# Mean over rows of 32 KiB: one load queue with one row per descriptor, in place of two queues with two adjacent rows per descriptor

## The chip, the cores and the metric

The kernel runs on one NeuronCore of a Trainium2 chip. The metric is the device time of one execution in microseconds (us); for the kernel before it is 1252.54 us, the median of three runs (1252.18 to 1252.76). The engines are named as in the profile: DVE is VectorE, ACT is ScalarE, SP is SyncE, PE is TensorE, POOL is GpSimd; a name with a q (SPq, ACTq) is an engine's instruction queue, and PEld is TensorE's weight load. DMA queue q1 carries what SyncE issues, q10 what ScalarE issues.

## The reference

The input `x` has the shape 64 x 256 x 8192 in float32 (536.87 MB). The output is the mean over the last axis, 64 x 256 values:

```python
def reference(x):
    return np.mean(x, axis=2)
```

Seen as a matrix, there are 16,384 rows of 8192 numbers (32 KiB each), and each row gives one number. Every input byte is read once and used in one addition.

## The kernel before, in words

The rows are cut into NB = 64 blocks of 256 rows, 8 MiB each. A block is a tile `xt` of 128 partitions x R = 2 rows x 8192 columns. The view `x_v` says which row goes where: with `(n p r) s -> n p r s`, partition p of block n holds rows 2p and 2p+1 of the block, which are adjacent in memory, so that one partition's share is a single run of 64 KiB.

**Bulk.** LB = 63 blocks go through a pool of three buffers (`BULK_BUFS`). `load(n)` (line 71) issues one DMA for a whole block, on SyncE's queue for even n and on ScalarE's for odd n. Three loads are issued ahead; after that, load n+3 is issued right after the two sums of block n, whose buffer it takes. `dve_sum` (line 61, a VectorE tensor_reduce) sums row 0 of each partition into a column of `res[0]`; `act_sum` (line 64, a ScalarE activation with an accumulator that writes its copy back over the input) sums row 1 into a column of `res[1]`. A load into a used buffer waits for both sums of the block that was there.

**Last block.** It uses a fourth turn of the same pool. Row 0 of all partitions is one DMA (line 91, 4 MiB); its left half is summed on VectorE and its right half on ScalarE, into the two columns of `head`. Row 1 is loaded in chunks of 4096, 2048, 1024 and 512 columns (line 97), each halved between the two engines, whose sums go to columns of `fin_in`; the last 512 columns are loaded straight into `fin_in` (line 106) behind the others on SyncE's queue.

**Results.** Line 108 multiplies the two parts of `head` by 1/8192 and adds them up, into `fin`. The 63 columns of `res[0]` and `res[1]` are each transposed on TensorE (line 121) and scaled into `bulk` on VectorE (line 122), and stored with one DMA (line 123) issued by SyncE. Line 125 scales the last 512 columns and the eight partial sums beside them and adds them up on VectorE, and line 134 stores the last block's 256 means.

The framework that builds the program orders the instructions of each engine itself, and so a line of the source can run earlier than its place: on VectorE one of the two operations of line 122 runs ahead of the sum of `head`, the other behind it, and the sums of the chunks follow line 108. Within an engine's queue the order is then fixed, and an instruction that waits holds up those behind it.

Of the kernel before, what the change touches and what calls it, by code (L numbers as in the profile page):

```python
# [1 line left out]

# [4 lines left out]

ROWS = 2
BULK_BUFS = 3
LAST_CHUNKS = (4096, 2048, 1024, 512, 512)  # L10


@with_exitstack
def kernel(
    ctx: ExitStack,
    tc: tile.TileContext,
    x: bass.AP,
    out: bass.AP,
):
    nc = tc.nc  # L20
    P = nc.NUM_PARTITIONS
    F32 = mybir.dt.float32
    X = mybir.AxisListType.X
    ADD = mybir.AluOpType.add
    COPY = mybir.ActivationFunctionType.Copy

    B, C, S = x.shape
    N = B * C
    R = ROWS
    assert R == 2 and N % (P * R) == 0, (N, P, R)  # L30
    NB = N // (P * R)
    LB = NB - 1
    assert 1 <= LB <= P and sum(LAST_CHUNKS) == S
    inv = 1.0 / float(S)

    x_v = x.rearrange("b c s -> (b c) s").rearrange("(n p r) s -> n p r s", p=P, r=R)
    o_v = out.rearrange("b c -> (b c)")
    out_bulk = o_v[0 : LB * P * R].rearrange("(n p r) -> n p r", p=P, r=R)
    out_last = o_v[LB * P * R : N].rearrange("(p r) -> p r", r=R)

    in_pool = ctx.enter_context(tc.tile_pool(name="in", bufs=BULK_BUFS))
    res_pool = ctx.enter_context(tc.tile_pool(name="res", bufs=1))
    psum_pool = ctx.enter_context(
        tc.tile_pool(name="psum", bufs=1, space=bass.MemoryType.PSUM)
    )

    res = [res_pool.tile([P, NB], F32, name=f"res{r}") for r in range(R)]
    ident = res_pool.tile([P, P], F32)
    nc.gpsimd.memset(ident[:], 0.0)  # L49
    nc.gpsimd.affine_select(  # L50
        out=ident[:],
        in_=ident[:],
        compare_op=mybir.AluOpType.not_equal,
        fill=1.0,
        base=0,
        pattern=[[-1, P]],
        channel_multiplier=1,
    )

    def dve_sum(dst, src):  # L60
        nc.vector.tensor_reduce(out=dst, in_=src, axis=X, op=ADD)  # L61

    def act_sum(dst, src):
        nc.scalar.activation(out=src, in_=src, func=COPY, accum_out=dst)  # L64

    queues = [nc.sync, nc.scalar]
    loaded = {}

    def load(n):
        xt = in_pool.tile([P, R, S], x.dtype, name="xt")  # L70
        queues[n % 2].dma_start(out=xt[:], in_=x_v[n])
        loaded[n] = xt

    for n in range(min(BULK_BUFS, LB)):
        load(n)
    for n in range(LB):
        xt = loaded.pop(n)
        dve_sum(res[0][:, n : n + 1], xt[:, 0, :])
        act_sum(res[1][:, n : n + 1], xt[:, 1, :])
        if n + BULK_BUFS < LB:  # L80
            load(n + BULK_BUFS)

    nparts = 2 * len(LAST_CHUNKS)
    lastw = LAST_CHUNKS[-1]
    xl = in_pool.tile([P, R, S], x.dtype, name="xt")
    fin_in = res_pool.tile([P, lastw + nparts], F32)
    fin = res_pool.tile([P, R], F32)
    head = res_pool.tile([P, 2], F32)

    half = S // 2  # L90
    nc.sync.dma_start(out=xl[:, 0, :], in_=x_v[LB, :, 0, :])
    dve_sum(head[:, 0:1], xl[:, 0, 0:half])
    act_sum(head[:, 1:2], xl[:, 0, half:S])

    pos, k = 0, 0
    for c, w in enumerate(LAST_CHUNKS[:-1]):
        ld = nc.sync.dma_start(
            out=xl[:, 1, pos : pos + w], in_=x_v[LB, :, 1, pos : pos + w]
        )
        mid = pos + w // 2  # L100
        dve_sum(fin_in[:, lastw + k : lastw + k + 1], xl[:, 1, pos:mid])
        act_sum(fin_in[:, lastw + k + 1 : lastw + k + 2], xl[:, 1, mid : pos + w])
        k += 2
        pos += w
    with tc.issue_after(ld.ins):
        nc.sync.dma_start(out=fin_in[:, 0:lastw], in_=x_v[LB, :, 1, pos:S])

    nc.vector.tensor_scalar(  # L108
        out=head[:],
        in0=head[:],  # L110
        scalar1=inv,
        scalar2=None,
        op0=mybir.AluOpType.mult,
        op1=ADD,
        accum_out=fin[:, 0:1],
    )

    bulk = res_pool.tile([P, P, R], F32)
    for r in range(R):
        ps = psum_pool.tile([P, P], F32, name=f"ps{r}")  # L120
        nc.tensor.transpose(out=ps[:LB, :], in_=res[r][:, 0:LB], identity=ident[:])  # L121
        nc.vector.tensor_scalar_mul(out=bulk[:LB, :, r], in0=ps[:LB, :], scalar1=inv)  # L122
    nc.sync.dma_start(out=out_bulk, in_=bulk[:LB])

    nc.vector.tensor_scalar(  # L125
        out=fin_in[:, 0 : lastw + k],
        in0=fin_in[:, 0 : lastw + k],
        scalar1=inv,
        scalar2=None,
        op0=mybir.AluOpType.mult,  # L130
        op1=ADD,
        accum_out=fin[:, 1:2],
    )
    nc.sync.dma_start(out=out_last, in_=fin[:])


# [1 line left out]
_INS = ['x']  # L138
_OUTS = [((64, 256), 'float32')]


# [23 lines left out]
```

## Time and profile before

| what | value |
|---|---|
| median of three runs | 1252.54 us |
| the profiled execution's own time | 1252.76 us |
| its span, first to last instruction | 1251.0 us |
| VectorE busy | 555.6 us (44%) |
| ScalarE busy | 457.8 us (37%) |
| one sum of 8192 columns on VectorE | 8.684 us, 63 of them |
| one sum of 8192 columns on ScalarE | 7.030 us, 63 of them |
| VectorE waiting for loads | 690.4 us |
| ScalarE waiting for loads | 782.5 us |
| DMA packets | 10156, 536.97 MB, 429 GB/s over the span |
| queue q1 (SyncE) | 5688 packets, 276.89 MB |
| queue q10 (ScalarE) | 4464 packets, 260.05 MB |
| a bulk load on SyncE, issue to landing | 39.6 us (median of 32) |
| a bulk load on ScalarE, issue to landing | 36.2 us (median of 31) |
| the last store, issue to landing | 3.3 us |

How to read it: "busy" is the time in which an engine executes; waiting for a load is idle time that ended with a DMA's landing. The time from issue to landing holds the wait behind earlier transfers and the sharing with the other queue, not only the transfer. A packet is one piece that one of the 16 DMA engines moves; the share of a DMA queue is the time that its packets took, over the time of 16 engines. The difference between the profiled execution's time and its span, 1.76 us, lies around the program.

### The profile page before, as it was taken

What the parts mean: (1) busy time and instruction counts of PE and PEld (TensorE: products, weight loads), DVE (VectorE), ACT (ScalarE), POOL (GpSimd) and SP (SyncE); (2) the same over time, 40 slices, a digit from 0 to 9 for tenths busy, and PEclk for the clock granted to TensorE, in tenths of its full rate; (3) what the DMA queues carried; (4) which work ended last, traced back from release to release, by engine and by line L of the source; (5) the groups of instructions that cost most, each with busy time, mean ns of one, the idle gap of its engine ahead of it and who ended that gap; (6) DMA issues with size and microseconds to landing.
All of it is one profiled execution on the core that took longest, in us unless ns stands there. A gap on an engine that the chain in (4) does not pass through costs nothing. (4 is left out here: it accounts for less than half of the span.)

```text
span 1251.0 us, 434 instructions
## 1 busy us (share of the span) xinstructions
PE 0.7 (0%) x2; PEld 0.3 (0%) x2; DVE 555.6 (44%) x74; ACT 457.8 (37%) x137; POOL 0.7 (0%) x6
## 2 busy tenths in 40 slices
PE   0000000000000000000000000000000000000000
PEld 0000000000000000000000000000000000000000
DVE  0525543345433455333553335543255432555338
ACT  0424432234422344322443224442244422444226
POOL 0000000000000000000000000000000000000000
DMA  9999999999999999999999999999999999999997
GB/s 402 436 436 436 436 436 436 436 436 423 423 427 436 436 436 436 436 436 436 436 436 434 436 427 423 425 436 436 436 436 436 436 434 436 434 434 436 436 419 294
DMA packets 10156, 536.97 MB, mean 429 GB/s; under 512 B 1257, under 2 KB 1320, under 8 KB 1704
## 3 DMA queue, kind: packets, MB, share of 16 engines
q1 hardware_dynamic: 5688, 276.89, 51.3%
q10 hardware_dynamic: 4464, 260.05, 48.1%
q14 instruction: 4, 0.03, 0.0%
HBM read 536.87 MB, written 0.07 MB: 429 GB/s over the span
## 5 line engine op out<-in xcount | busy, mean ns | idle before, releaser
L61 DVE TENSOR_REDUCE res<-xt 128x1 f32<-128x8192 f32 x63 | 545.7, 8684 | 690.4 <-DMA xt<-in_x_dram 690.4
L64 ACT ACTIVATE xt<-xt 128x8192 f32<-128x8192 f32 (+2 forms) x68 | 450.5, 6625 | 784.5 <-DMA xt<-in_x_dram 782.5
L64 ACT ACTIVATION_READ_ACCUMULATOR xt<-xt 128x1 f32 x68 | 12.7, 187 | 0.0
L61 DVE TENSOR_REDUCE head<-xt 128x1 f32<-128x4096 f32 x1 | 4.4, 4402 | 0.0
L61 DVE TENSOR_REDUCE fin_in<-xt 128x1 f32<-128x2048 f32 (+3 forms) x4 | 4.3, 1144 | 0.0
L64 ACT ACT_TABLE_LOAD x1 | 1.3, 1283 | 1.2 <-PEq L149 1.2
L121 PE MATMUL ps<-ident,res 128*63 128x128 f32 x2 | 0.7, 433 | 1236.3 <-DVE res L61 1236.3
L122 DVE TENSOR_SCALAR bulk<-ps 63x128 f32<-63x128 f32 x2 | 0.6, 278 | 0.6 <-PE ps L121 0.6
L125 DVE TENSOR_SCALAR_CACHE_REDUCE fin_in<-fin_in 128x520 f32<-128x520 f32 x1 | 0.7, 694 | 0.1
L121 PEld LDWEIGHTS ps<-ident,res 128*63 128x63 f32 x2 | 0.3, 205 | 1236.3 <-issue 1236.3
L50 POOL TENSOR_SCALAR_AFFINE_SELECT ident<-ident 128x128 f32<-128x128 f32 x1 | 0.3, 294 | 0.1
L49 POOL MEMSET ident<- 128x128 f32 x1 | 0.2, 205 | 0.3 <-POOLq L149 0.3
L108 DVE TENSOR_SCALAR_CACHE_REDUCE head<-head 128x2 f32<-128x2 f32 x1 | 0.2, 155 | 0.0
L149 POOL MEMSET const-bfloat16-1.0<- 128x1 bf16 x1 | 0.1, 102 | 0.0
L149 POOL MEMSET const-uint8-127<- 128x1 uint8 x1 | 0.1, 102 | 0.0
L149 POOL MEMSET const-float32-0.0<- 128x1 f32 x1 | 0.1, 99 | 0.2 <-issue 0.2
L149 POOL MEMSET const-float32-1.0<- 128x1 f32 x1 | 0.1, 99 | 0.0
L108 DVE DVE_READ_ACCUMULATOR head<-head 128x1 f32 x1 | 0.1, 83 | 0.0
L125 DVE DVE_READ_ACCUMULATOR fin_in<-fin_in 128x1 f32 x1 | 0.1, 82 | 0.0
## 6 DMA issues: line engine op xcount, KB each, us to landing
xt<-in_x_dram SPq DMA_DIRECT2D x1, 4096.0 KB, 35.0
xt<-in_x_dram SPq DMA_DIRECT2D x1, 2048.0 KB, 39.5
xt<-in_x_dram SPq DMA_DIRECT2D x1, 1024.0 KB, 41.6
xt<-in_x_dram SPq DMA_DIRECT2D x32, 39.6
xt<-in_x_dram SPq DMA_DIRECT2D x1, 512.0 KB, 42.4
xt<-in_x_dram ACTq DMA_DIRECT2D x31, 36.2
xt<-in_x_dram SPq DMA_DIRECT2D x1, 256.0 KB, 42.5
fin_in<-in_x_dram SPq DMA_DIRECT2D x1, 256.0 KB, 42.7
```

The costliest lines, as they stand in the source:

```text
L49: nc.gpsimd.memset(ident[:], 0.0)
L50: nc.gpsimd.affine_select(out=ident[:], in_=ident[:], compare_op=mybir.AluOpType.not_equal, fill=1.0, base=0, pattern=[[-1, P]], channel_m ...
L61: nc.vector.tensor_reduce(out=dst, in_=src, axis=X, op=ADD)
L64: nc.scalar.activation(out=src, in_=src, func=COPY, accum_out=dst)
L108: nc.vector.tensor_scalar(out=head[:], in0=head[:], scalar1=inv, scalar2=None, op0=mybir.AluOpType.mult, op1=ADD, accum_out=fin[:, 0:1],)
L121: nc.tensor.transpose(out=ps[:LB, :], in_=res[r][:, 0:LB], identity=ident[:])
L122: nc.vector.tensor_scalar_mul(out=bulk[:LB, :, r], in0=ps[:LB, :], scalar1=inv)
L125: nc.vector.tensor_scalar(out=fin_in[:, 0 : lastw + k], in0=fin_in[:, 0 : lastw + k], scalar1=inv, scalar2=None, op0=mybir.AluOpType.mult, ...
L149: nc = _bacc.Bacc("TRN2", target_bir_lowering=False, num_devices=1)
```

## The change

The view of the input becomes `(n r p) s -> n p r s`: partition p of a block holds rows p and 128+p, two runs of 32 KiB that lie 4 MiB apart. The views of the output follow. All loads are issued by SyncE; the load of a block stands in the loop ahead of its two sums, and the three buffers alone decide how far ahead of the sums it is issued. `bulk` becomes 128 x 2 x 128 with the row index outside, so that line 122 writes contiguous columns. The chunks of the last block, the sums and the number of buffers stay.

```diff
-    x_v = x.rearrange("b c s -> (b c) s").rearrange("(n p r) s -> n p r s", p=P, r=R)
+    x_v = x.rearrange("b c s -> (b c) s").rearrange("(n r p) s -> n p r s", p=P, r=R)
     o_v = out.rearrange("b c -> (b c)")
-    out_bulk = o_v[0 : LB * P * R].rearrange("(n p r) -> n p r", p=P, r=R)
-    out_last = o_v[LB * P * R : N].rearrange("(p r) -> p r", r=R)
+    out_bulk = o_v[0 : LB * P * R].rearrange("(n r p) -> n r p", p=P, r=R)
+    out_last = o_v[LB * P * R : N].rearrange("(r p) -> p r", r=R)
...
-    queues = [nc.sync, nc.scalar]
-    loaded = {}
-
-    def load(n):
+    for n in range(LB):
         xt = in_pool.tile([P, R, S], x.dtype, name="xt")
-        queues[n % 2].dma_start(out=xt[:], in_=x_v[n])
-        loaded[n] = xt
-
-    for n in range(min(BULK_BUFS, LB)):
-        load(n)
-    for n in range(LB):
-        xt = loaded.pop(n)
+        nc.sync.dma_start(out=xt[:], in_=x_v[n])
         dve_sum(res[0][:, n : n + 1], xt[:, 0, :])
         act_sum(res[1][:, n : n + 1], xt[:, 1, :])
-        if n + BULK_BUFS < LB:
-            load(n + BULK_BUFS)
...
-    bulk = res_pool.tile([P, P, R], F32)
+    bulk = res_pool.tile([P, R, P], F32)
...
-        nc.vector.tensor_scalar_mul(out=bulk[:LB, :, r], in0=ps[:LB, :], scalar1=inv)
+        nc.vector.tensor_scalar_mul(out=bulk[:LB, r, :], in0=ps[:LB, :], scalar1=inv)
```

## The prediction

> **What bounds the kernel now.** I read the page's 40 slices and queues first, then the chain of waits, the timeline of the tail, and last the DMA packets of two short windows in which one queue is alone.
>
> The slices and the queues say what the span is made of:
>
> ```profile
> DMA  9999999999999999999999999999999999999997
> ...
> HBM read 536.87 MB, written 0.07 MB: 429 GB/s over the span
> ```
>
> The DMA engines are never idle; VectorE is busy 44% and ScalarE 37%, and both stand waiting for loads (690.4 and 782.5 us). The stream's steady rate is read from the timeline of VectorE:
>
> ```profile
> 1141.47 17.28 DVE L61 TENSOR_REDUCE res<-xt 128x1 f32<-128x8192 f32 x2 [20.34 <-DMA xt<-in_x_dram]
> ...
> 1177.77 8.69 DVE L61 TENSOR_REDUCE res<-xt 128x1 f32<-128x8192 f32 x1 [19.01 <-DMA xt<-in_x_dram]
> ...
> 1189.86 8.69 DVE L61 TENSOR_REDUCE res<-xt 128x1 f32<-128x8192 f32 x1 [3.40 <-DMA xt<-in_x_dram]
> ...
> 1218.89 17.28 DVE L61 TENSOR_REDUCE res<-xt 128x1 f32<-128x8192 f32 x2 [20.35 <-DMA xt<-in_x_dram]
> ```
>
> Four blocks take 77.42 us, 19.35 us each. The pattern is uneven because two queues share the engines: two blocks come close together ("x2" is two sums without a gap), then one, then one. The last such pair is at the very end, and there it costs something. The chain that ended last is short:
>
> ```profile
> 1245.05 0.92 DVE fin_in L61 x2
> 1245.97 0.11 issue
> 1246.08 0.69 DVE fin_in L125
> ```
>
> These are sums on VectorE, not a transfer. The last chunk (issued at 1200.89, 42.7 us to landing) was there at 1243.59, so L125 starts 2.49 us after its data:
>
> ```profile
> 1237.01 4.40 DVE L61 TENSOR_REDUCE head<-xt 128x1 f32<-128x4096 f32 x1
> ...
> 1241.64 4.33 DVE L61 TENSOR_REDUCE fin_in<-xt 128x1 f32<-128x2048 f32 x4
> ```
>
> VectorE is behind: blocks 61 and 62 keep it until 1236.2, so `head`, whose row landed at 1233.62, starts at 1237.01, and four sums run without a gap.
>
> The change sets the size of a packet, so its price is needed. Queue lines give packets, MB and the share of 16 engines' time. First the 64 KiB packets between 42 and 50 us, SyncE's queue alone, then the 32 KiB packets of the last block's first row between 1223 and 1227.9 us:
>
> ```profile
> q1 hardware_dynamic: 48, 3.15, 90.8%
> ```
>
> ```profile
> q1 hardware_dynamic: 64, 2.06, 97.8%
> ```
>
> 0.908 x 16 x 8 us / 48 = 2.4213 us for 64 KiB. One of the 64 in the second line is a semaphore write (9 ns in the packet records), so 0.978 x 16 x 4.9 us / 63 = 1.2169 us for 32 KiB, or 2.4338 us for two.
>
> **The change part by part.** All sums are made against the profiled execution: 1252.76 us, of which the span is 1251.0. It is the highest of three; the median is 1252.54, so 0.22 us come off at the end.
>
> *Packets of the bulk loads.* Partition p held rows 2p and 2p+1, one 64 KiB run; now it holds rows p and 128+p, two runs of 32 KiB. The ScalarE queue shows 4464 packets for 31 loads: 144 each, 128 with data and 16 semaphore writes, hence 8 data packets per engine and block. They become 16. Over 63 blocks that is 63 x 8 = 504 more on every engine, in the stream that sets the span. Two 32 KiB packets last 2.4338 - 2.4213 = 12.5 ns longer than one of 64 KiB. But durations overlap: eight of 2.4213 and a semaphore write make 19.38 us where the measured block takes 19.35, about 3 ns per packet, which an added packet saves too. That leaves 9.5 ns. The start-to-start distances that I chained together from the packet records agree: 2.418 us for 64 KiB, 1.214 for 32 KiB, 10 ns per pair. So 504 x 9.9 ns = +5.0 us. Ends: 0 if the boundary is hidden in the new order, and 26 ns, +13.1 us, if long packets are as common as between 1225 and 1230 us, where the same row shows 97.9% for 64 packets, 1.224 us each (one took 1.59). I take 9.9, since 110 of the 112 distances between 32 KiB packets lie between 1.209 and 1.225 us.
>
> The Trainium skill ("DMA: Bandwidth & Descriptors", Why small descriptors are slow) gives a packet a fixed overhead of about 3 cycles; with its 850 MHz fabric clock I estimate 3.5 ns, 1.8 us over 504, and a sum of 1251.9 instead of 1255.2. The measured row is nearly three times that, and I go by the row.
>
> *Address order.* The two runs of a partition now lie 4 MiB apart. The nearest row is the phase with both queues: there an engine's successive packets come from blocks 8 MiB apart, and between 500 and 600 us the ScalarE queue's 320 data packets (368 less 48 semaphore writes) average 2.424 us, 2 ns over the single-queue figure. So +0.0, with 504 x 2 = 1.0 us as an upper end.
>
> The skill speaks against this part: the same page (Latency and other measured facts, HBM row pitch at large powers of two) measured copies at 103 GB/s with a row pitch of 4 MiB against 214 with padding. That would double the span. It concerns the pitch from partition to partition, which here falls from 64 to 32 KiB; no run here shows a load that alternates over 4 MiB.
>
> *One queue in place of two.* The 31 issues on ScalarE (0.33 us each) go; SyncE issues 63 loads. They cost nothing: ScalarE waits 782.5 us for loads anyway. On SyncE, load n+3 waits for both sums of block n, 8.7 us after its landing; queued behind are only later loads. At that point block n+1 has some 10.6 us to run and n+2 is queued whole, so the issue has about 30 us to spare. The engines go on at full rate with one queue (the 42 to 50 us line), so no gap is added between blocks: successive DMAs of one queue are separated by a 6 ns semaphore write in the last block. Bounds: -1.2 us (504 x 2.3 ns, single-queue against two-queue packets above, counted for the 504 packets that remain), and +63 x 0.1 = 6.3 us if each hand-over cost what the chunk of 2048 columns shows over the proportion of its bytes (landings at 1238.5 and 1241.05: 2.5 us against 2.42). I take 0.
>
> *The tail.* In one queue block 62 is alone in front of the last block, and 61 lands a whole block, 19.4 us, before it. Row 0 landed at 1233.62, and its 4 MiB take 9.7 us, so 62 lands near 1223.9. VectorE then sums 8.69 us, to 1232.6; `head` starts with its landing and ends at 1238.1; the sum of 4096 columns starts at 1238.5 and takes 2.29; then 1.21 from 1241.05, 0.68, 0.41, each about when its chunk lands, and L125 starts near 1243.65 instead of 1246.08. -2.4 us. Late next is the last chunk's transfer, which keeps its size. The two L122 (0.28 each), their matmuls and L108 fall in the 1.0 us before `head` and the 0.4 after it; if they all came last they would cost 0.8. Ends: -2.45 and 0.
>
> *The stores.* The bulk store keeps 63 runs of 1 KB; it is issued earlier but behind the last chunk in the same queue. L122 now writes contiguous columns, off the path. The final store takes 256 elements of 4 bytes in place of 128 of 8: its window shows 144 packets within 0.2 us and 3.3 us to landing, so 128 more cost 0.1 to 0.2; upper end another 3.3, if landing doubled. I take +0.1.
>
> **Sum:** 1252.76 + 5.0 + 0.0 + 0 - 2.4 + 0.1 = 1255.46; less 0.22 for the median, **1255.2 us**, 0.2% slower. 0.2%, 2.5 us, is about what a measurement of this kernel can tell from no change, so the forecast sits close to that edge.
>
> **The rivals.**
> - *The boundary is cheap* (0 to 4 ns). For: semaphore writes cost only 6 ns; against: the 32 KiB row. 504 x 4 ns = 2.0, and 1252.54 + 2.0 - 2.3 = 1252.2; at 0 ns 1250.2.
> - *Faster:* nothing is added by the packets, and the lone queue's 2.3 ns per packet is a gain all along: 1252.54 - 2.3 - 1.2 = 1249.0. It decides when the boundary costs less than the queue saves. Against it: the single-queue window is short, and shares have one decimal.
> - *Long packets or the 4 MiB stride:* 26 ns per pair, 1252.54 + 13.1 - 2.3 = 1263.3; a part of it gives 1258 to 1263.
> - *The backlog stays:* if the order of VectorE's work puts the small operations or `head` late, the 2.4 us are not won: 1252.54 + 5.0 + 0.1 = 1257.6.
>
> **How the numbers follow.** Forecast 0.55 (its own range 1253.8 to 1257.2, two thirds of it above 1255.04); cheap boundary 0.17, nearly all of it within 0.2%; faster 0.08; long packets 0.15; backlog 0.05. Slower: 0.37 + 0.15 + 0.05 = 0.57. Same: 0.18 + 0.15 = 0.33. Faster: 0.08 + 0.02 = 0.10. Range 1250.3, the free boundary, to 1259.0, which takes in the backlog and the milder part of the long packets.
>
> **What will show it.** One sum of 8.69 us every 19.43 us in place of the uneven pattern, with some 49 us from issue to landing; some 8190 more packets (504 x 16, and 128 of the last store); two packets of 32 KiB at 2.43 us in a bulk window. In the tail, waits for DMA before `head` and before each chunk's sum, and a chain that ends over a transfer. I am wrong if the block takes 19.35 us or less, if blocks show gaps between them, or if VectorE still runs `head` and the chunks without a wait.

## The result, and the profile after

The changed kernel takes 1259.97 us (median of four runs, 1259.75 to 1260.09) against 1252.44 us before (four runs, one more than in the table above): a ratio of 1.0060, 95% interval 1.0042 to 1.0077. That is 7.5 us slower; 1255.2 was forecast, with a range to 1259.0. The profiled execution took 1260.04 us, its span is 1258.3.

The page of the changed kernel, its slices, packets and loads:

```profile
DMA  9999999999999999999999999999999999999996
...
DMA packets 18348, 536.97 MB, mean 427 GB/s; under 512 B 1385, under 2 KB 1448, under 8 KB 1832
...
xt<-in_x_dram SPq DMA_DIRECT2D x63, 8192.0 KB, 49.5
```

The DMA engines are still never idle until the end, and a load lands 49.5 us after its issue: the queue always holds work. The timeline of VectorE, in the bulk and in the tail (start, duration, what; in brackets the idle time before and what ended it):

```profile
1189.25 8.69 DVE L61 TENSOR_REDUCE res<-xt 128x1 f32<-128x8192 f32 x1 [10.74 <-DMA xt<-in_x_dram]
...
1208.68 8.69 DVE L61 TENSOR_REDUCE res<-xt 128x1 f32<-128x8192 f32 x1 [10.74 <-DMA xt<-in_x_dram]
...
1228.10 8.69 DVE L61 TENSOR_REDUCE res<-xt 128x1 f32<-128x8192 f32 x1 [10.74 <-DMA xt<-in_x_dram]
...
1237.84 4.42 DVE L61 TENSOR_REDUCE head<-xt 128x1 f32<-128x4096 f32 x1 [0.20 <-DMA xt<-in_x_dram]
...
1247.90 0.69 DVE L114 TENSOR_SCALAR_CACHE_REDUCE fin_in<-fin_in 128x520 f32<-128x520 f32 x1 [0.35 <-DMA fin_in<-in_x_dram]
```

One block every 19.43 us, evenly; `head` waits for its row, and the last sum (L114 here, L125 before) waits for the last chunk. So far all is as the prediction has it. The surprise is the line of the last store, from its DMA list and from the packets between 1248 us and the end:

```profile
out_dram<-fin SPq DMA_DIRECT2D x1, 1.0 KB, 8.7
```

```profile
DMA  0000005000000000000000000000000000000000
...
DMA packets 272, 0.00 MB, mean 0 GB/s; under 512 B 272, under 2 KB 272, under 8 KB 272
```

In the kernel before, the same store stands so:

```profile
out_dram<-fin SPq DMA_DIRECT2D x1, 1.0 KB, 3.3
```

The same 1 KB, in 256 pieces with 16 semaphore writes, takes 8.7 us from issue to landing instead of 3.3. All 272 packets fall into one slice of 0.26 us, near 1249.7; the remaining 7.6 us to the landing at 1257.3 show no packet at all. The 7.3 us of the span are put together from these places:

| from | before | after | difference |
|---|---|---|---|
| start to the landing of the last chunk | 1243.59 | 1247.78 | +4.2 |
| landing of the last chunk to the last sum | 2.49 | 0.12 | -2.4 |
| last sum to the issue of the last store | 0.73 | 0.73 | 0 |
| issue of the last store to its landing | 3.3 | 8.7 | +5.4 |
| from there to the end of the span | 0.9 | 1.0 | +0.1 |

### The profile page after: what moved, and what is told of

Read it like the earlier page. It is cut to its first block, busy times and chain, and to the rows that moved or that the text cites. A ratio compares the mean times of both kernels' runs of the same rounds, so it can differ in the third digit from the quotient of the medians.

```text
span 1258.3 us, 464 instructions
## 1 busy us (share of the span) xinstructions
PE 0.9 (0%) x2; PEld 0.4 (0%) x2; DVE 557.5 (44%) x74; ACT 458.0 (36%) x137; POOL 0.7 (0%) x6
## 4 chain that ended last, share of the span: by engine, by line
DMA 82%; DVE 15%; another core or an unknown queue 2%; SPq 0%; issue 0%; DVEq 0%
DMA xt<-in_x_dram 78%; DVE res L61 15%; DMA fin_in<-in_x_dram 4%; SPq L86 0%; SPq L68 0%; DVE fin_in L114 0%; SPq L80 0%; DVEq L114 0%; DVEq L149 0%
## 5 line engine op out<-in xcount | busy, mean ns | idle before, releaser
L114 DVE TENSOR_SCALAR_CACHE_REDUCE fin_in<-fin_in 128x520 f32<-128x520 f32 x1 | 0.7, 695 | 0.3 <-DMA fin_in<-in_x_dram 0.3
L114 DVE DVE_READ_ACCUMULATOR fin_in<-fin_in 128x1 f32 x1 | 0.1, 83 | 0.0
## 6 DMA issues: line engine op xcount, KB each, us to landing
xt<-in_x_dram SPq DMA_DIRECT2D x63, 8192.0 KB, 49.5
```

The costliest lines, as they stand in the source:

```text
L114: nc.vector.tensor_scalar(out=fin_in[:, 0 : lastw + k], in0=fin_in[:, 0 : lastw + k], scalar1=inv, scalar2=None, op0=mybir.AluOpType.mult, ...
```

## The experiments

After the result there are two things to settle. First, why the last store lands late: theory S puts it down to its 4-byte pieces, rival Q to the single queue. Second, whether the slower stream comes from the size of the packets (theory P) or from the single queue (Q2) or the order of addresses (A, with the 4 MiB alternation). The medians below stand against the kernel before as it was measured beside them: 1251.92 us for e1 to e4, 1251.99 for e6 and e7, 1251.91 for e8, e9 and e11.

| run | packets, queue | us | ratio, 95% interval | us per block | last store, us to landing |
|---|---|---|---|---|---|
| e1_after_8b_store | 32 KiB, one | 1254.05 | 1.0018 [1.0009, 1.0027] | 19.43 | 2.9 |
| e2_before_4b_store | 64 KiB, two | 1257.17 | 1.0041 [1.0028, 1.0055] | 19.35, uneven as before | 7.6 |
| e3_64k_one_queue | 64 KiB, one | 1249.87 | 0.9982 [0.9974, 0.9991] | 19.35 | 3.0 |
| e4_32k_two_queues | 32 KiB, two | 1255.31 | 1.0028 [1.0017, 1.0039] | 38.86 for two | 2.9 |
| e6_32k_adjacent | 32 KiB, one | 1254.81 | 1.0022 [1.0013, 1.0032] | 19.42 | 3.0 |
| e7_16k | 16 KiB, one | 1264.60 | 1.0101 [1.0087, 1.0115] | 19.58 | 3.2 |
| e8_last_store_rows | 64 KiB, one | 1248.59 | 0.9973 [0.9962, 0.9983] | 19.35 | not listed |
| e9_64b_runs | 64 KiB, one | 1248.40 | 0.9971 [0.9960, 0.9983] | 19.35 | 1.4 |
| e11_64k_one_queue_again | 64 KiB, one | 1249.59 | 0.9981 [0.9972, 0.9990] | 19.35 | 2.8 |

**The store put back in the changed kernel, and put alone into the kernel before.** Each edit touches the last block only.

```diff
 # e1: the changed kernel
+    x_l = x.rearrange("b c s -> (b c) s").rearrange("(n p r) s -> n p r s", p=P, r=R)
-    out_last = o_v[LB * P * R : N].rearrange("(r p) -> p r", r=R)
+    out_last = o_v[LB * P * R : N].rearrange("(p r) -> p r", r=R)
...
 # and the loads of the last block from x_l[LB, ...]; e2 is the reverse edit in the kernel before
```

> The changed kernel with the last block alone put back to rows 2p and 2p+1, so that the final store writes 128 runs of 8 bytes again; bulk and queue as changed. Theory S (the final store of 256 four-byte pieces costs the 5.4 us by which its landing grew from 3.3 to 8.7 us): 1259.97 - 5.4 = 1254.6 us, landing of the last store near 3.3 us. Rival Q (the store lands late because everything went through one queue, whatever its pieces are): 1260.0 us, landing near 8.7 us.

> The kernel before with the last block alone in the new row order, so that the final store writes 256 pieces of 4 bytes; bulk loads of 64 KiB on two queues as before. Theory S: 1252.44 + 5.4 = 1257.8 us, landing of the last store near 8.7 us. Rival Q: 1252.4 us, landing near 3.3 us.

Theory S holds in both directions. With the 8-byte store the changed kernel takes 1254.05 us, and its last store, between 1248 and 1253 us, lands like the one of the kernel before:

```profile
q1 hardware_dynamic: 144, 0.00, 1.5%
...
out_dram<-fin SPq DMA_DIRECT2D x1, 1.0 KB, 2.9
```

The kernel before with the 4-byte store goes the other way, by 1257.17 - 1251.92 = 5.25 us, though it has two queues and 64 KiB packets:

```profile
out_dram<-fin SPq DMA_DIRECT2D x1, 1.0 KB, 7.6
```

This landing is 4.3 us later than the 3.3 of the kernel before, and not the 8.7 that I expected; a landing of this kind varies by more than a microsecond from kernel to kernel. Against the kernel before beside each, the store is worth 7.53 - 2.13 = 5.4 us in the changed kernel (e1) and 5.25 in the old one (e2), and so no part of it shows for the number of load queues. Both edits change the row order of the last block's loads too; e5, below, has the two stores without these loads.

**Packet size and queue taken apart.**

```diff
 # e3: the kernel before
-    queues = [nc.sync, nc.scalar]
+    queues = [nc.sync, nc.sync]
```

```diff
 # e4: the kernel before
-    x_v = x.rearrange("b c s -> (b c) s").rearrange("(n p r) s -> n p r s", p=P, r=R)
+    x_v = x.rearrange("b c s -> (b c) s").rearrange("(n r p) s -> n p r s", p=P, r=R)
...
 # the last block in the old order; out_bulk and bulk as in the changed kernel
```

> The kernel before with all loads issued by SyncE, 64 KiB packets and 8-byte store kept. Theory P (the slower stream comes from the size of the packets, and one queue alone costs nothing and takes the backlog of VectorE out of the tail): a block every 19.35 us, the last sum starts 2.4 us earlier, 1250.0 us. Rival Q2 (the slower stream, 19.43 us per block, comes from the single queue): the stream is 4 to 5 us longer, 1254 to 1255 us.

> The kernel before with the bulk blocks in the new row order (two 32 KiB runs per partition), still on two queues in turn; the last block and its 8-byte store as before. Theory P: 504 more packets per engine at about 9 ns add 4 to 5 us, and the backlog in the tail stays: 1256.5 to 1257.5 us, four blocks in 77.7 us. Rival Q2: 1252.4 us, four blocks in 77.4 us.

One queue with 64 KiB packets is 2.05 us faster than before: a block every 19.35 us, and VectorE waits for `head` and for the last chunk, where it was behind in the kernel before:

```profile
1204.52 8.69 DVE L61 TENSOR_REDUCE res<-xt 128x1 f32<-128x8192 f32 x1 [10.66 <-DMA xt<-in_x_dram]
1223.87 8.69 DVE L61 TENSOR_REDUCE res<-xt 128x1 f32<-128x8192 f32 x1 [10.66 <-DMA xt<-in_x_dram]
...
1233.59 4.42 DVE L61 TENSOR_REDUCE head<-xt 128x1 f32<-128x4096 f32 x1 [0.19 <-DMA xt<-in_x_dram]
...
1243.95 0.69 DVE L125 TENSOR_SCALAR_CACHE_REDUCE fin_in<-fin_in 128x520 f32<-128x520 f32 x1 [0.34 <-DMA fin_in<-in_x_dram]
```

Two queues with 32 KiB packets slow the stream just as one queue does: 38.86 us for two blocks. The time, 1255.31, lies 1.2 us below the lower end of what was expected. Half a microsecond of this is the level of the kernel before, 1251.92 beside this run against the 1252.44 that I had reckoned from. For the rest, the pattern of the two queues is another: the loads land in regular pairs, and the last pair leaves VectorE less far behind. Its last chunk was issued at 1202.59 and landed 45.2 us later, at 1247.79, and the last sum starts here:

```profile
1182.96 17.28 DVE L62 TENSOR_REDUCE res<-xt 128x1 f32<-128x8192 f32 x2 [21.58 <-DMA xt<-in_x_dram]
1221.82 17.28 DVE L62 TENSOR_REDUCE res<-xt 128x1 f32<-128x8192 f32 x2 [21.58 <-DMA xt<-in_x_dram]
...
1248.99 0.69 DVE L126 TENSOR_SCALAR_CACHE_REDUCE fin_in<-fin_in 128x520 f32<-128x520 f32 x1
```

That is 1.2 us after its data instead of 2.5. Why the pattern changed is not shown; what the backlog cost at the end differed with it.

**The price of a packet, without the 4 MiB alternation and at a second size.**

```diff
 # e6, on e3
-        queues[n % 2].dma_start(out=xt[:], in_=x_v[n])
+        for r in range(R):
+            queues[n % 2].dma_start(out=xt[:, r, :], in_=x_v[n, :, r, :])
 # e7, on e3
+        for h in range(2):
+            c = slice(h * S // 2, (h + 1) * S // 2)
+            queues[n % 2].dma_start(out=xt[:, :, c], in_=x_v[n, :, :, c])
```

> The kernel before on SyncE's queue alone, each block in two loads, one per row of the partitions: 32 KiB packets in the old row order, no 4 MiB alternation, 8-byte store. Theory P (size alone sets the price): 504 more packets per engine as in the changed kernel and 63 more semaphore writes of 6 ns: with the tail of one queue, 1250.0 + 4.5 + 0.4 = 1254.9 us, 19.43 to 19.44 us per block. Rival A (the 4 MiB alternation costs something): nearer to 1250.4 us, 19.36 us per block.

> The kernel before on SyncE's queue alone, each block in two loads of half the columns: packets of 16 KiB, 32 per engine and block in place of 8; 8-byte store. Theory P with a fixed price per packet: 24 x 63 = 1512 more packets per engine at 9 ns add 13.6 us to 1250.0, 1263.6 us, 19.57 us per block. Rival: the price is not per packet but belongs to what changed in the order of addresses: below 1256 us.

Over e3, whose 1249.87 us are taken as the base: e6 adds 4.9 us, of which 63 more semaphore writes of 6 ns are 0.4, so 4.5 us / 504 = 9 ns for a packet more. The changed rows in e1 add 4.2 us, 8 ns each, and its block takes as long as that of e6 (19.43 and 19.42 us): no cost of the alternation over 4 MiB shows beyond the size. e7 adds 14.7 us, 14.3 without the semaphore writes, and 14.3 / 1512 = 9.5 ns. The blocks of e7 agree:

```profile
1042.54 8.69 DVE L61 TENSOR_REDUCE res<-xt 128x1 f32<-128x8192 f32 x1 [10.90 <-DMA xt<-in_x_dram]
1062.11 8.69 DVE L61 TENSOR_REDUCE res<-xt 128x1 f32<-128x8192 f32 x1 [10.88 <-DMA xt<-in_x_dram]
```

19.58 us against 19.35, 0.23 us for 24 more packets. Size and number of packets explain the stream; Q2 and A fall.

**The store by itself.** Two kernels hold only stores of a small tile; between two of them VectorE changes the tile, and so each store is alone.

```diff
 # e5, one line per shape, for example
+        nc.sync.dma_start(out=o[0:K].rearrange("(p r) -> p r", r=2), in_=src[:, 0:2])
...
+        nc.sync.dma_start(out=o[0:K].rearrange("(r p) -> p r", r=2), in_=src[:, 0:2])
 # e10, pieces of z bytes every d bytes, written here for all shapes at once
+        nc.sync.dma_start(out=o[0 : P * d // 4].rearrange("(p r) -> p r", r=d // 4)[:, 0 : z // 4], in_=src[:, 0 : z // 4])
```

> Only stores, each alone and three times, after a small load; the sums are left out and the output is not the mean. Times from issue to landing. Theory C (pieces of 4 bytes that share a stretch of memory with other engines' pieces wait for each other): 128 or 256 pieces of 4 bytes close together land late, 6 to 9 us, the same 256 pieces 256 bytes apart land in about 3 us, like 128 pieces of 8 bytes. Rival N (the number of pieces under some size sets it): 256 pieces land at 6 to 9 us wherever they lie, 128 pieces at about 3 us. Rival B (4 bytes is slow by itself): 128 pieces of 4 bytes land late at any distance. Two runs of 512 bytes: 2 to 3 us by all of them.

> Only stores again, 128 pieces of 4, 8, 16 or 32 bytes at steps of 4 to 64 bytes, each alone and three times; the sums are left out. Theory C with 64 bytes as the stretch that is shared: the landing falls with the number of pieces per 64 bytes: 9 us at 16 pieces (4 bytes, step 4), 3 to 4.5 us at 8, 2 to 2.5 us at 4, below 2 us at 2 and 1.4 us at 1, whatever the size of a piece. Rival: the size of a piece decides, and 4 bytes at a step of 32 still take over 3 us.

Medians of three, us from issue to landing (marked *: the wait of VectorE for the landing, where the list of DMAs gives no time, of three and of two values):

| pieces | e5 | e10 |
|---|---|---|
| 256 of 4 bytes, the order of the changed kernel | 9.0 | |
| 128 of 4 bytes, step 4 | 9.3* | 7.1 |
| 128 of 4 bytes, step 8 | 4.3 | 3.6 |
| 128 of 8 bytes, step 8, the order of the kernel before | 3.2 | 3.0 |
| 128 of 4 bytes, step 16 / 32 / 64 | 1.4 (step 64) | 1.4 / 1.4 / 1.4 |
| 128 of 4 / 8 bytes, step 512 | 1.4 / 1.4 | |
| 128 of 8 bytes, step 16 / 32 | | 1.4 / 1.4 |
| 128 of 16 bytes, step 16 / 32 | | 1.9 / 1.5 |
| 128 of 32 bytes, step 32 | | 1.4 |
| 256 of 4 bytes, step 256 | 1.9 | |
| 128 of 64 / 512 bytes, dense | 1.9 / 1.5 | |
| 2 of 512 bytes | 1.2* | |

For the two orders of this change, lines 36 and 39 of e5 give:

```profile
DMA to landing us min/median/max: 2.9/3.2/3.6
```

```profile
DMA to landing us min/median/max: 8.9/9.0/9.1
```

For 128 pieces of 4 bytes, lines 41 (step 8) and 46 (step 16) of e10 give:

```profile
DMA to landing us min/median/max: 3.2/3.6/3.9
```

```profile
DMA to landing us min/median/max: 1.4/1.4/1.7
```

Among the stores at wider steps, single values reach 2.7 us, and so 1.9 is not clearly later than 1.4.

Neither the number of pieces nor their size decides: 256 pieces of 4 bytes far apart land in 1.9 us (I had expected 3), and 128 of 4 bytes in 1.4 us once they are 16 bytes apart. What they have in common is closeness, theory C, but not with the smooth fall that I expected: for four pieces in 64 bytes I had put 2 to 2.5 us, and 1.4 was measured (1.9 with pieces of 16 bytes). The drop lies between a step of 8 bytes and one of 16, that is, between eight and four pieces per 64 bytes. The 64 bytes were my assumption, and no run shows that memory is shared in stretches of this length. Size is not quite without a part: at a step of 8 bytes, pieces of 4 bytes land 0.6 to 1.1 us later than pieces of 8. The Trainium skill ("DMA: Bandwidth & Descriptors", The descriptor swizzle) says of a transfer to 128 partitions that four neighbouring partitions belong to one DMA engine. If a store is divided in the same way, which no run here shows, a stretch of 64 bytes with four pieces is one engine's, and one with more is shared. That would fit, but no run here has four neighbours of different engines, and so it stays open whether the number of pieces or that of the engines counts, and what the landing waits for.

**Cheaper last stores on e3.** e8 turns the last block's 256 means into two rows on TensorE; e9 regroups the blocks so that every partition ends with 16 adjacent results.

```diff
 # e8, the last block in the order (n r p)
...
-    nc.sync.dma_start(out=out_last, in_=fin[:])
...
+    nc.tensor.transpose(out=ps_f[:R, :], in_=fin[:, 0:R], identity=ident[:])
...
+    nc.vector.tensor_copy(out=rows[:R, :], in_=ps_f[:R, :])
+    nc.sync.dma_start(out=out_last, in_=rows[:R])
 # e9
+    x_g = x.rearrange("b c s -> (b c) s").rearrange("(g p m r) s -> g m p r s", g=G, m=M, r=R)
+    out_last = o_v[(G - 1) * K : N].rearrange("(p j) -> p j", p=P)
...
 # block n is x_g[n // 8, n % 8]; res is scaled into bulk and fin without transposes
```

> 64 KiB packets on one queue, the last block in the new row order, its 256 means turned on TensorE and copied by VectorE, so that the final store writes 2 runs of 512 bytes. The store alone with 2 runs landed 1.2 us after its issue against 3.0 for 128 runs of 8 bytes; the detour is one matmul (0.45 us), one copy (0.28) and two hand-overs (about 0.4), some 1.1 us in all. Theory C (closeness of small pieces sets the landing): 1249.9 - 1.8 + 1.1 = 1249.2 us. Rival (a landing near 3 us belongs to any store at the end of this kernel): 1251.0 us.

> 64 KiB packets on one queue, the blocks regrouped so that a partition holds 16 adjacent rows over 8 blocks: no transposes, the stores write runs of 64 bytes, the last one 128 of them; in the input, neighbouring partitions now lie 512 KiB apart. Theory C: the last store lands in 1.4 to 1.9 us instead of 3.0, 1249.9 - 1.3 = 1248.6 us, if the stream keeps 19.35 us per block. Rival H (a pitch of 512 KiB slows the loads): every 0.1 us more per block adds 6.3 us; the Trainium skill's table (DMA: Bandwidth & Descriptors, Latency and other measured facts) has 207 GB/s at that pitch against 214, from which I estimate 3% more, near 1290 us.

> 64 KiB packets on one queue with the 8-byte store, a second time beside the two kernels above: 1249.9 us as in the run before, by all theories.

Beside 1249.59 us for e11, e8 takes 1248.59 and e9 1248.40, 3.3 and 3.5 us less than the kernel before. e9's chain and the last store's line:

```profile
1243.31 0.07 issue
1243.38 0.69 DVE fin_in L114
```

```profile
out_dram<-fin SPq DMA_DIRECT2D x1, 8.0 KB, 1.4
```

From the issue of the last store to the end of the span it is 2.3 us in e9 and 1.9 in e8, 3.7 in e11, 4.2 in the kernel before and 9.7 in the changed one; from the start of the last sum to the issue of the store it takes 1.48 us in e8, with the matmul and the copy, and 0.73 in e11. e9's blocks still take 19.35 us with partitions 512 KiB apart: rival H falls, and the Trainium skill's figures on row pitch ("DMA: Bandwidth & Descriptors", Latency and other measured facts), which it came from, do not carry over to these loads of 64 KiB runs.

Put together, the changed kernel differs from the one before by three things: one queue, -2.05 us (e3); 32 KiB packets, +4.2 (e1 over e3); and the 4-byte store, +5.4. Their sum is the 7.5 us measured, as it must be, since e3 and e1 are steps on one way from the old kernel to the new; e2 (5.25 for the store) and e6 (4.5 for the packets) come to about the same prices from elsewhere.

## Why the prediction was wrong

The step that failed is "the final store takes 256 elements of 4 bytes in place of 128 of 8 ... I take +0.1", with 3.3 as the upper end. It measured 5.4 us between the two profiles; e1 and e2 confirm it from both sides, with 5.4 and 5.25 us. The step counted packets, whose starts had taken 0.2 us, and doubled them. But some 2.3 of the 3.3 us in the kernel before lay after the last packet's start, and no row showed what they were made of; a rise of that part was not bounded by doubling it. The runs show in its place that the landing goes by how close the small pieces lie. This cost also lies bare at the end, with no work beside it, and so was not to be passed over with a small number.

The other terms stand. The stream was priced at +5.0 us and grew by 4.2 to the last landing; the packet was priced at 9.9 ns and costs 8 to 9.5. The 3 cycles of the Trainium skill ("DMA: Bandwidth & Descriptors", Why small descriptors are slow), from which I estimated 3.5 ns, make up less than half of that. The alternation over 4 MiB was put at 0 and costs nothing that e1 and e6 can show. The single queue was put at 0 in the stream, and e3 shows no gap: 19.35 us per block. The tail was put at -2.4 us and gave -2.4 (2.49 to 0.12). Forecast without the store, 1255.2 - 0.1 is 1255.1, or 2.6 us over the kernel before; e1, which is the change without its store, took 1254.05, 2.1 over the kernel before beside it.

The direction was right, and not by the store alone, since e1 is slower too. Of the rivals the cheap boundary, the faster one and the lasting backlog did not come. The time fell near the rival of the long packets, but not by its cause: they are not more frequent, since a block takes 19.43 us throughout.

## What to carry to other kernels

In a kernel that is bound by its loads, what follows the last landing is worth as much as the stream: here the new layout of a store of 1 KB cost more (5.4 us) than 8064 more packets (4.2). Price a last store by how its pieces lie in memory, not by its bytes or packets, and lay the results out in longer runs if the rows can be regrouped: runs of 64 bytes (e9) and two of 512 (e8) saved 1.0 to 1.2 us over runs of 8. Two queues brought no rate here (19.35 us per block, as with one), but made loads land unevenly or in pairs; one queue in order let the last sum keep up with the last load and saved 2.05 us (2.3 in e11).

## What the runs showed of the hardware that was not expected

Small pieces written close together delay the landing far beyond their transfer: in e10, 128 pieces of 4 bytes land in 7.1 us at a step of 4 bytes, 3.6 at 8 and 1.4 at 16. A packet more in a load of the same bytes costs 8 to 9.5 ns, at 32 and at 16 KiB alike. Neither an alternation over 4 MiB nor a pitch of 512 KiB between partitions changed the rate of the loads.
